# Where the streamed tiles of a transformer block's matmuls begin in on-chip memory: from one offset for all to steps of 32 bytes

## The chip, the cores and the metric

The kernel is one program on one core of one Trainium2 chip. A core has a matmul engine (TensorE, PE in the profile, with its weight loads as PEld), a vector engine (VectorE, DVE), a scalar engine (ScalarE, ACT), a general engine (GpSimd, POOL) and an engine that issues transfers (SyncE, SP). They share an on-chip memory of 128 partitions; sums of products are built up in a second one, the accumulator memory. The metric is device time in microseconds, from the first to the last instruction of the core; lower is better.

## The reference

The computation is one layer of a diffusion block in float32, for one sequence of 512 tokens of 2048 features, with a context of 256 tokens. Cut to what matters here:

```python
sh1, sc1, g1, sh2, sc2, g2 = split(silu(c) @ w_ada + b_ada)      # modulation; the same for the context
h  = rmsnorm(x + pos, norm_mix_pre) * (1 + sc1) + sh1            # [512, 2048]
z, xbc, dt, hy = split(h @ w_in)                                 # 2048 -> 5664
y  = concat([ssd(z, xbc, dt, context), hyena(hy)]) @ w_out       # 2048 -> 2048
x  = x + pos + g1 * rmsnorm(y, norm_mix_post)
h  = rmsnorm(x, norm_ffn_pre) * (1 + sc2) + sh2
x  = x + g2 * rmsnorm((silu(h @ w_gate) * (h @ w_up)) @ w_down, norm_ffn_post)   # 2048 -> 5632 -> 2048
```

Nearly all arithmetic lies in the products with `w_in`, `w_out`, `w_gate`, `w_up` and `w_down`.

## The kernel before

**Tiles.** Features lie on the 128 partitions and tokens along them, so a tensor of 2048 features is 16 blocks `k`, each a tile of 128 x 512 (2048 bytes in a partition). A product is taken in float32 with split operands: `x = xh + xl` and `w = wh + wl`. For each block, `mm3` issues three matmuls into one accumulator: `wh` against `xh`, `wh` against `xl`, `wl` against `xh`. In each the weights (128 x 128) are loaded into the array, and the tile of `x` is streamed through it; this text calls it the moving tile. `gemm` goes through the 16 blocks in order, so that two pieces of weights of 8 blocks each make one output tile.

**Names.** The moving tiles have several names over the program, in the same slots: `hh`/`hl` (the normed input), `mh`/`ml` (the mixed output before `w_out`) and `fh`/`fl` (the input of the feed-forward part) are tiles of pool `big`, tags `h0` to `h15` and `l0` to `l15`. `ah`/`al` are the activations that `w_down` takes: six slots each in pool `fa`. `ch`/`cl` are the context, 256 tokens. A few pieces of weights that are used twice go into slots of `big` as well (`bhi`/`blo`, by `wload_big`).

**Weights.** `wload` brings a raw piece of 128 x 1024 by a transfer from SP, ScalarE casts it to `whi` and VectorE (GpSimd in the start) makes `wlo`; raw, `whi` and `wlo` have three buffers each. A piece is split two pieces ahead of its use (`push`).

**Order.** The program's order is written out by hand. Products follow each other; small steps of other work (norms, the state-space part, the transforms of the long convolution, the later modulation vectors) are generators in the lists `urgent` and `fillers`, of which `pump` runs some after every fourth block. Each engine then takes its instructions in order, except for what the build may move where two tiles of different lifetimes share memory: a tile that needs the place of an earlier one waits until that one is released.

**Places in memory.** Pools are laid out one behind the other, on the left side upwards: `cst` (constants), `big`, `wp` (weights), `rsm`, and above them the pools of each part. As built, before the change, every tile of `big` begins at 96 modulo 256 bytes of a partition, and so do `raw`, `whi` and `wlo`, with a slice of weights every 512 bytes; `ah`, `al`, `ch` and `cl` begin at 32 modulo 256.

Of the kernel before, what the change touches and what calls it, by code (L numbers as in the profile page):

```python
# [46 lines left out]
# columns of the packed per-feature vectors  # L47
# [17 lines left out]
def block_kernel(ctx: ExitStack, tc: tile.TileContext, I: dict, out: bass.AP, dbg=None, stop=None):  # L65
# [32 lines left out]

    uniq = [0]
# [18 lines left out]
    mod = cst.tile([128, 8, 16], F32, name="mod")  # L118
    nc.gpsimd.memset(ones, 1.0)
# [4 lines left out]
    hh = [big.tile([128, 512], F32R, tag=f"h{k}", name=f"hh{k}") for k in range(KT)]  # L124
    hl = [big.tile([128, 512], F32R, tag=f"l{k}", name=f"hl{k}") for k in range(KT)]
    hx = [(hh[k], hl[k]) for k in range(KT)]

# [38 lines left out]
    def wload_big(ap, q):  # L166
        """Into the slots of four blocks of features that are free meanwhile."""
        raw = wraw(ap)
        parts = []
        for i in range(2):  # L170
            o = i * 512
            hi = big.tile([128, 512], F32R, tag=f"h{q * 2 + i}", name=nm("bhi"))
            lo = big.tile([128, 512], F32R, tag=f"l{q * 2 + i}", name=nm("blo"))
            split(hi, lo, raw[:, o : o + 512])
            parts += [(hi[:, c : c + 128], lo[:, c : c + 128]) for c in range(0, 512, 128)]
        return parts
# [11 lines left out]
    # a piece is split some pieces before its products are issued  # L188
# [11 lines left out]
    def flush(nxt=()):  # L200
        """Issue what waits; the first pieces of the next part are split meanwhile."""
        nxt = list(nxt)
        while ahead or nxt:
            if nxt:
                stash.append(wload(nxt.pop(0)))
            if ahead:
                w, fn = ahead.pop(0)
                fn(w)
# [28 lines left out]
    class Sumsq:  # L237
        """Sum over the features of the squares, by partitions first; the last ones go to the PE alone."""
# [91 lines left out]
    # mod slots: shift and scale of x, then of ctx; the four later sections of x  # L330
# [6 lines left out]
    # =====================================================================  # L337
    # start: x + pos, its norm, and h by blocks of features as w_ada arrives;
    # six tiles of the first GEMM take each block as it comes
    # =====================================================================  # L340
# [11 lines left out]
    # silu(c) and silu(c_ctx) on every partition  # L352
# [22 lines left out]
    # the scales, of x and ctx at once: rows of w_ada on the PE  # L375
# [22 lines left out]
    # the shifts: silu(c) and silu(c_ctx) against transposed blocks of w_ada  # L398
# [11 lines left out]
    # sums of squares: half of the features on the PE, the others on DVE first  # L410
# [56 lines left out]
    # =====================================================================  # L467
    # xbc of x, and the first hyena inputs; beside them the modulation of ctx
    # =====================================================================
# [57 lines left out]
    def u_out(pv, px, j):  # L527
# [10 lines left out]
        # folded again: sums and differences of the even, then of the odd part  # L538
# [17 lines left out]
    # ctx: norm and modulation  # L556
# [23 lines left out]
    # dt: of x from the third tile of the start  # L580
# [42 lines left out]
    # =====================================================================  # L623
    # ctx: dt and its part of the xbc GEMM
    # =====================================================================
# [25 lines left out]
    def softplus():  # L651
        # softplus(x) = max(x, 0) + log1p(e), e = exp(-|x|); log1p(e) = 2 atanh(e / (2 + e))
# [46 lines left out]
    def hb8(ap):  # [128, 8] over heads of 64  # L699
        return ap.unsqueeze(2).broadcast_to([128, 8, 64])  # L700
# [4 lines left out]
    def decayed(td, x, c, d, g):  # dt * x, with the decay up to the end of the chunk  # L705
        o = d * 16 + g * 8
        tt(nc.gpsimd, v8(td), v8(x), hb8(dd[:, c, o : o + 8]), MUL)
        return td
# [11 lines left out]
    # =====================================================================  # L720
    # SSD, beside the GEMMs of the hyena inputs
    # =====================================================================
# [45 lines left out]
    # the steps of dt * A in two parts of 12 bits, and masks of ones that both parts meet exactly  # L768
# [13 lines left out]
    # of four heads: the terms of the sums of dt * A, and dt of the direction that a pair of steps belongs to  # L782
# [16 lines left out]
    def ssd():  # L799
        for g in range(2):  # L800
# [19 lines left out]
            for c in range(4):  # L820
# [20 lines left out]
                for q4 in range(2):  # L841
                    # the exponents of both directions do not meet: one is zero where the other is not
# [68 lines left out]
    # =====================================================================  # L911
    # z, the gate of the SSD output; beside it the transform of the hyena
    # filter, by quarters of the channels
    # =====================================================================
# [68 lines left out]
    def filt():  # L983
        for q in range(4):
# [20 lines left out]
            # h1 at t = 0 is in the norm, but not in the filter  # L1005
# [6 lines left out]
            # times t and 512 - t meet: sums serve the even cosines and odd sines,  # L1012
            # differences the others; the first row holds the times 0 and 256
# [43 lines left out]
    mh = [big.tile([128, 512], F32R, tag=f"h{k}", name=f"mh{k}") for k in range(KT)]  # L1057
    mlo = [big.tile([128, 512], F32R, tag=f"l{k}", name=f"ml{k}") for k in range(KT)]
# [4 lines left out]
    # the norm's factor of each token multiplies the product with w_out instead  # L1063
# [6 lines left out]
    # =====================================================================  # L1070
    # w_out, the SSD half of the sum; beside it the hyena: x1 * v, its
    # transform, product, inverse; then * x0
    # =====================================================================
# [13 lines left out]
    def chain():  # L1087
        for q in range(4):
# [6 lines left out]
            for m in range(4):  # L1095
                pc = aux()
                for s, tab in ((0, ucos), (1, usin)):
                    # even frequencies meet only the sums or only the differences
# [66 lines left out]
    # =====================================================================  # L1165
    # w_out, the hyena half, by halves of the tokens; beside it and the first
    # FFN tiles: residual, norm and modulation before the FFN
    # =====================================================================
# [4 lines left out]
    posc = fa.tile([128, 512], F32, tag="ah", bufs=NA, name="posc")  # L1173
    pos = pos_load(jn, posc.rearrange("p (k c) -> p k c", k=8))
# [13 lines left out]
    def junction(h, prs):  # L1188
# [10 lines left out]
        for k in range(KT):  # L1199
            if h == 0:  # L1200
                fx[k] = (big.tile([128, 512], F32R, tag=f"h{k}", name=f"fh{k}"),
                         big.tile([128, 512], F32R, tag=f"l{k}", name=f"fl{k}"))
            modulated(fx[k][0][:, sl], fx[k][1][:, sl], yT[k][:, sl], a2[:, k : k + 1], mod[:, 5, k : k + 1], rx[:, sl], 256)
            yield
# [20 lines left out]
    # the second half takes first the pieces that are still there from the first  # L1225
# [15 lines left out]
    # =====================================================================  # L1241
    # FFN
    # =====================================================================
    acts = {}

    def gate_up(i, c0, c1):
# [3 lines left out]
        def up_done(pu):  # L1250
            if i not in acts:
                h = fa.tile([128, 512], F32R, tag="ah", bufs=NA, name=nm("ah"))
                l = fa.tile([128, 512], F32R, tag="al", bufs=NA, name=nm("al"))
# [72 lines left out]
    # the pieces stay for the second half: most in the place of the FFN's input  # L1326
# [14 lines left out]
def _constants():  # L1341
# [4 lines left out]
    def emb(n):  # L1346
        a = (np.arange(n, dtype=f)[:, None] * om).astype(np.float64)
        return np.concatenate([np.sin(a), np.cos(a)], -1).astype(f)  # [n, 1024]
# [11 lines left out]
    # times 0 .. 255, then 256, 511, 510, ... 257  # L1360
# [7 lines left out]
    # frequencies: multiples of 4, the other even ones, the odd ones  # L1368
# [11 lines left out]
    ph = (m.T * (2 * tp[None, :] + 1)) % 2048  # [m, t'], in units of pi / 1024  # L1380
# [4 lines left out]
    for name, u in (("cos", uc), ("sin", us)):  # L1385
        near, far = u[:, :128], u[:, :127:-1]
        odd = [x[lo : lo + 128] / 2 for lo in (256, 384) for x in (near + far, near - far)]
        blocks = np.stack([near[:128], near[128:256]] + odd, 0)  # [block, m, t]
# [6 lines left out]
def _layout(a):  # L1395
# [4 lines left out]
    def stat(w):  # [K, N] -> [N/128, K/1024, 128, 8 * 128]  # L1400
# [3 lines left out]
    def cols(v):  # [n * 128] -> [128, n]  # L1404
# [12 lines left out]
    # [pc, k2, 128, sec, g, 512] -> [sec, g, pc, 128, k2, 512]  # L1417
    wa = a["w_ada"][0]
    R["ada2"] = wa.reshape(8, 2, 128, 6, 4, 512).transpose(3, 4, 0, 2, 1, 5).reshape(6, 4, 8, 128, 1024)[1:]
    # the first section transposed: [half, 1024, k, 128] -> [k, half, 128, 1024]  # L1420
# [3 lines left out]
    # [chunk, k4, 128, q, s, 128] -> [chunk, q, 128, s, k4, 128]  # L1424
# [30 lines left out]
```

## Time and profile before

| | |
|---|---|
| time, median of 2 runs | 2626.44 us (2624.69 to 2628.19) |
| the profiled execution, first to last instruction | 2627.0 us, the execution's own time as the trace has it |
| matmuls / share of the span that PE is busy | 12196 / 96% |
| weight loads (PEld) | 78% |
| VectorE, ScalarE, GpSimd | 56%, 29%, 17% |
| transfers | 388.52 MB, mean 148 GB/s |

Matmuls are pipelined: the record of one lasts longer than the step from its start to the start of the next, and it is this step that adds up to the time. A step is therefore read from the starts in the timeline, as the difference of two starts over the number of matmuls between them, and not from the mean duration in a group of instructions.

### The profile page before, as it was taken

What the parts mean: (1) busy time and instruction counts of PE and PEld (TensorE: products, weight loads), DVE (VectorE), ACT (ScalarE), POOL (GpSimd) and SP (SyncE); (2) the same over time, 40 slices, a digit from 0 to 9 for tenths busy, and PEclk for the clock granted to TensorE, in tenths of its full rate; (3) what the DMA queues carried; (4) which work ended last, traced back from release to release, by engine and by line L of the source; (5) the groups of instructions that cost most, each with busy time, mean ns of one, the idle gap of its engine ahead of it and who ended that gap; (6) DMA issues with size and microseconds to landing.
All of it is one profiled execution on the core that took longest, in us unless ns stands there. A gap on an engine that the chain in (4) does not pass through costs nothing.

```text
span 2627.0 us, 30945 instructions
## 1 busy us (share of the span) xinstructions
PE 2525.5 (96%) x12196; PEld 2050.2 (78%) x12196; DVE 1471.1 (56%) x1889; ACT 758.2 (29%) x1062; POOL 454.2 (17%) x421
## 2 busy tenths in 40 slices
PE   8999999899999999999999999999999999999996
PEld 3467779577767788889888888888888888888886
DVE  7986756888878766696334343434343333333336
ACT  3143325222123322454322222222222222222224
POOL 1230010565523245740000000000000000000005
PEclk9999999899999999999999999999999999999998
DMA  8867644445356666345433333333333333333232
GB/s 288 317 211 237 224 159 167 145 147 162 112 196 209 245 223 221 103 147 185 145 112 112 108 110 112 112 111 112 112 112 105 96 96 96 96 96 94 95 103 80
DMA packets 129354, 388.52 MB, mean 148 GB/s; under 512 B 13775, under 2 KB 34703, under 8 KB 127672
## 3 DMA queue, kind: packets, MB, share of 16 engines
q1 hardware_dynamic: 129208, 386.54, 44.9%
q8 instruction: 96, 1.57, 0.2%
q14 instruction: 50, 0.41, 0.0%
HBM read 367.09 MB, written 19.40 MB: 147 GB/s over the span
## 4 chain that ended last, share of the span: by engine, by line
PE 54%; DVE 2%; issue 0%; POOL 0%; ACT 0%; POOLq 0%; DVEq 0%; ACTq 0%
PE acc L82 54%; DVE y2a L79 1%; DVE wlo L79 1%; DVE yTa L76 0%; POOL gs L79 0%; DVE yTa L79 0%; DVE fl L76 0%; PE aux L82 0%; DVE mt L76 0%; ACT whi L162 0%; PE aux L234 0%; POOL r L79 0%; POOL yTa L79 0%; ACT sq L73 0%; ACT dg L73 0%
## 5 line engine op out<-in xcount | busy, mean ns | idle before, releaser
L162 ACT CAST whi<-raw 128x1024 fp32r<-128x1024 f32 (+1 forms) x436 | 452.9, 1039 | 1424.2 <-PE acc L82 1185.3
L79 DVE TENSOR_TENSOR wlo<-raw,whi 128x1024 fp32r<-128x1024 f32 x420 | 530.8, 1264 | 544.4 <-ACT whi L162 540.5
L82 PE MATMUL acc<-fh,wlo 128*128 128x512 f32 (+1 forms) x1600 | 581.9, 364 | 5.3 <-DVE wlo L79 5.3
L82 PE MATMUL acc<-fh,whi 128*128 128x512 f32 (+1 forms) x1600 | 582.4, 364 | 0.1
L82 PE MATMUL acc<-fl,whi 128*128 128x512 f32 (+1 forms) x1600 | 581.9, 364 | 0.1
L82 PEld LDWEIGHTS acc<-fh,wlo 128*128 128x128 f32 x1600 | 301.8, 189 | 53.8 <-DVE wlo L79 6.1
L82 PEld LDWEIGHTS acc<-fl,whi 128*128 128x128 f32 x1600 | 301.8, 189 | 47.8 <-DVE fl L76 0.3
L82 PEld LDWEIGHTS acc<-fh,whi 128*128 128x128 f32 x1600 | 301.8, 189 | 47.8 <-ACT fh L73 0.3
L79 POOL TENSOR_TENSOR gs<-gs,sq 128x256 f32<-128x256 f32 x91 | 85.6, 944 | 1457.6 <-ACT sq L73 1454.1
L82 PE MATMUL acc<-hh,whi 128*128 128x512 f32 x688 | 287.0, 419 | 4.4 <-ACT hh L73 4.2
L82 PE MATMUL acc<-hl,whi 128*128 128x512 f32 x688 | 278.5, 405 | 2.8 <-DVE hl L76 2.8
L82 PE MATMUL acc<-hh,wlo 128*128 128x512 f32 x688 | 278.1, 404 | 0.0
L82 PE MATMUL acc<-ah,whi 128*128 128x512 f32 (+1 forms) x688 | 265.7, 386 | 0.0
L82 PE MATMUL acc<-ah,wlo 128*128 128x512 f32 (+1 forms) x688 | 265.5, 386 | 0.0
L82 PE MATMUL acc<-al,whi 128*128 128x512 f32 (+1 forms) x688 | 265.4, 386 | 0.0
L76 DVE SCALAR_TENSOR_TENSOR ada<-raw,cc,ada 128x512 f32<-128x512 f32 x240 | 200.5, 835 | 114.0 <-DMA raw<-in_ada 111.0
L79 DVE TENSOR_TENSOR y2a<-y2a,acc 128x512 f32<-128x512 f32 (+1 forms) x176 | 112.0, 638 | 210.5 <-PE acc L82 209.4
L82 PEld LDWEIGHTS acc<-hh,whi 128*128 128x128 f32 x688 | 135.0, 197 | 40.6 <-ACT hh L73 6.1
L82 PEld LDWEIGHTS acc<-hl,whi 128*128 128x128 f32 x688 | 135.3, 197 | 34.6 <-DVE hl L76 3.8
L82 PEld LDWEIGHTS acc<-hh,wlo 128*128 128x128 f32 x688 | 134.0, 195 | 34.6 <-issue 4.5
L82 PEld LDWEIGHTS acc<-ah,wlo 128*128 128x128 f32 x688 | 128.7, 187 | 29.8
L82 PEld LDWEIGHTS acc<-ah,whi 128*128 128x128 f32 x688 | 128.6, 187 | 29.7 <-ACT ah L179 0.2
(297 smaller groups left out, 3074.4 us busy)
## 6 DMA issues: line engine op xcount, KB each, us to landing
raw<-in_ada SPq DMA_DIRECT2D x128, 512.0 KB, 3.7
raw<-in_w_gate SPq DMA_DIRECT2D x100, 512.0 KB, 3.5
raw<-in_w_up SPq DMA_DIRECT2D x100, 512.0 KB, 3.5
raw<-in_w_down SPq DMA_DIRECT2D x88, 512.0 KB, 3.5
ada<-in_ada SPq DMA_DIRECT2D x64, 512.0 KB, 4.8
raw<-in_w_hy SPq DMA_DIRECT2D x44, 512.0 KB, 3.7
raw<-in_w_out SPq DMA_DIRECT2D x41, 512.0 KB, 4.0
raw<-in_w_xbc SPq DMA_DIRECT2D x38, 512.0 KB, 3.4
```

What stands on the lines that cost most here:

```text
L76: nc.vector.scalar_tensor_tensor(out=o, in0=a, scalar=s, in1=b, op0=op0, op1=op1)
L79: e.tensor_tensor(out=o, in0=a, in1=b, op=op)
L82: nc.tensor.matmul(o, lhsT, rhs, start=start, stop=stop)
L162: nc.scalar.copy(out=hi[:, :n], in_=raw[:, :n])
```

## The change

Every tile of `big`, and `ah` and `al`, is allocated 520 columns wide and used in its first 512, so that neighbouring tiles are 2080 bytes apart instead of 2048. Two small tiles that nothing uses (`pad0`, `pad1`) shift the pools behind them, and a scratch area at the foot of the memory, for descriptors of transfers that GpSimd would issue, is cut from 16 KB to 1 KB; no transfer of this kernel is issued there. As built, block `k` of `hh`, `hl`, `mh`, `ml`, `fh`, `fl` then begins at 32 `k` modulo 256; `raw`, `whi` and `wlo` begin at 0; slot `i` of `ah` begins at 32 `i`, of `al` at 192 + 32 `i`; `ch` and `cl` begin at 0. Comments are dropped too, which shifts line numbers by two.

```diff
+    rsm.tile([128, 16], F32, name="pad1")
...
     mod = cst.tile([128, 8, 16], F32, name="mod")
+    cst.tile([128, 40], F32, name="pad0")
...
-    hh = [big.tile([128, 512], F32R, tag=f"h{k}", name=f"hh{k}") for k in range(KT)]
-    hl = [big.tile([128, 512], F32R, tag=f"l{k}", name=f"hl{k}") for k in range(KT)]
+    hh = [big.tile([128, 520], F32R, tag=f"h{k}", name=f"hh{k}")[:, 0:512] for k in range(KT)]
+    hl = [big.tile([128, 520], F32R, tag=f"l{k}", name=f"hl{k}")[:, 0:512] for k in range(KT)]
...
-            hi = big.tile([128, 512], F32R, tag=f"h{q * 2 + i}", name=nm("bhi"))
-            lo = big.tile([128, 512], F32R, tag=f"l{q * 2 + i}", name=nm("blo"))
+            hi = big.tile([128, 520], F32R, tag=f"h{q * 2 + i}", name=nm("bhi"))[:, 0:512]
+            lo = big.tile([128, 520], F32R, tag=f"l{q * 2 + i}", name=nm("blo"))[:, 0:512]
... (the same for mh, ml, fh, fl)
-                h = fa.tile([128, 512], F32R, tag="ah", bufs=NA, name=nm("ah"))
-                l = fa.tile([128, 512], F32R, tag="al", bufs=NA, name=nm("al"))
+                h = fa.tile([128, 520], F32R, tag="ah", bufs=NA, name=nm("ah"))[:, 0:512]
+                l = fa.tile([128, 520], F32R, tag="al", bufs=NA, name=nm("al"))[:, 0:512]
...
-    nc = _bacc.Bacc("TRN2", target_bir_lowering=False, num_devices=1)
+    nc = _bacc.Bacc("TRN2", target_bir_lowering=False, num_devices=1, dynamic_dma_scratch_size=1024)
```

The matmuls keep their order, all of them, and so do VectorE's instructions. Between the start and the first products of `w_xbc` the pools on the left now overlap less with those on the right, and some instructions of the other engines change places.

GpSimd, where the start ends: `gs` is the running sum of squares of the context, `eo` and `f` are the folded hyena input, which TensorE transposes next. Before:

```order
L79 TENSOR_TENSOR gs_1530<-gs_1530,sq_1551 128x256
L79 TENSOR_TENSOR eo_1196<-hv_1186 128x256 x2
L79 TENSOR_TENSOR gs_1530<-gs_1530,sq_1556 128x256
L79 TENSOR_TENSOR f_267_1199<-eo_1196 128x2x128 x2
L79 TENSOR_TENSOR gs_1530<-gs_1530,sq_1635 128x256
L79 TENSOR_TENSOR gs_1530<-gs_1530,sq_1640 128x256
```

and now:

```order
L79 TENSOR_TENSOR gs_1532<-gs_1532,sq_1553 128x256
L79 TENSOR_TENSOR gs_1532<-gs_1532,sq_1558 128x256
L79 TENSOR_TENSOR gs_1532<-gs_1532,sq_1637 128x256
L79 TENSOR_TENSOR eo_1198<-hv_1188 128x256 x2
L79 TENSOR_TENSOR gs_1532<-gs_1532,sq_1642 128x256
L79 TENSOR_TENSOR f_267_1201<-eo_1198 128x2x128 x2
```

Two additions to `gs` now stand ahead of `f`.

ScalarE, at the same place: `whi` is a piece of weights, `xct` a tile of the context that has just been loaded. Before:

```order
L73 ACTIVATE ea<-bc 128x32
L162 CAST whi_1087<-raw_1085 128x1024
L73 ACTIVATE CT_1118<-acc_318,vec 128x512
L73 ACTIVATE CT_1119<-acc_319,vec 128x512
L73 ACTIVATE BT_1116<-acc_320,vec 128x512
```

and now:

```order
L73 ACTIVATE ea<-bc 128x32
L73 ACTIVATE gs_1532<-xct_1530 128x256
L73 ACTIVATE sq_1536<-xct_1534 128x256
L164 CAST whi_1089<-raw_1087 128x1024
L73 ACTIVATE CT_1120<-acc_320,vec 128x512
```

The first two squares of the context stand ahead of the second cast. SP issues the transfers of the context's tiles and of the masks a few places earlier there.

## Rows read from the trace of the kernel before

**Rows 1.** The page: PE's share, its 40 slices.
```profile
PE 2525.5 (96%) x12196; PEld 2050.2 (78%) x12196; DVE 1471.1 (56%) x1889; ACT 758.2 (29%) x1062; POOL 454.2 (17%) x421
...
PE   8999999899999999999999999999999999999996
```
**Rows 2.** A stretch: start:end, length; PE, PEld, DVE, ACT, POOL busy (count); PEclk, DMA.
```profile
1900.00:2000.00 100.00, 100.00 (x437) 81.58 (x436) 39.90 (x44) 21.44 (x23) 0.00 (x0) 1.00 0.34 107
```
**Rows 3.** Groups of PE's instructions by shape: count, busy us, mean ns, idle before.
```profile
L82 PE MATMUL acc<-fh,whi 128*128 128x512 f32 x1216 | 473.4, 389 | 0.0
...
L82 PE MATMUL acc<-hh,whi 128*128 128x512 f32 x688 | 287.0, 419 | 4.4 <-ACT hh L73 4.2 <-ACT hx L73 0.2
...
L82 PE MATMUL acc<-ah,whi 128*128 128x512 f32 x640 | 252.2, 394 | 0.0
...
L82 PE MATMUL acc<-fh,whi 128*128 128x256 f32 x384 | 108.9, 285 | 0.1
...
L82 PE MATMUL acc<-mh,whi 128*128 128x256 f32 x192 | 55.4, 289 | 1.4 <-DVE yTa L79 1.4
...
L82 PE MATMUL acc<-mh,whi 128*128 128x512 f32 x128 | 54.6, 426 | 0.0
...
L82 PE MATMUL acc<-ch,whi 128*128 128x256 f32 x176 | 50.2, 285 | 0.0
...
L82 PE MATMUL acc<-ah,bhi 128*128 128x256 f32 x80 | 22.5, 281 | 1.5 <-DVE y2a L79 1.5
...
L82 PE MATMUL acc<-mh,bhi 128*128 128x256 f32 x64 | 18.2, 284 | 0.0
...
L82 PE MATMUL acc<-ah,whi 128*128 128x256 f32 x48 | 13.5, 285 | 0.0
```
**Rows 4.** Timeline of PE, gate and up products: start us, length; 195 matmuls apart.
```profile
1854.93 0.39 PE L82 MATMUL acc<-fh,whi 128*128 128x512 f32 x1
...
1899.13 0.39 PE L82 MATMUL acc<-fh,whi 128*128 128x512 f32 x1
```
**Rows 5.** Timeline of PE, down products; 161 matmuls apart.
```profile
1812.25 0.39 PE L82 MATMUL acc<-ah,whi 128*128 128x512 f32 x1
...
1849.82 0.39 PE L82 MATMUL acc<-ah,wlo 128*128 128x512 f32 x1
```
**Rows 6.** Timeline of PE, gate and up by halves of the tokens; 166 matmuls apart.
```profile
1199.96 0.28 PE L82 MATMUL acc<-fl,whi 128*128 128x256 f32 x1
...
1219.88 0.28 PE L82 MATMUL acc<-fh,wlo 128*128 128x256 f32 x1
```
**Rows 7.** Timeline of PE, products of the context; 122 matmuls apart.
```profile
402.10 0.28 PE L82 MATMUL acc<-ch,wlo 128*128 128x256 f32 x1
...
415.93 0.28 PE L82 MATMUL acc<-cl,whi 128*128 128x256 f32 x1
```
**Rows 8.** Timeline of PE, start products 23 matmuls apart; the transposes of `f`.
```profile
183.67 0.39 PE L82 MATMUL acc<-hh,whi 128*128 128x512 f32 x1
...
188.88 0.39 PE L82 MATMUL acc<-hh,wlo 128*128 128x512 f32 x1
189.12 0.60 PE L548 MATMUL aux<-ident,f 128*128 128x128 f32 x4
```
**Rows 9.** Timeline of PE, products with w_out; 10 matmuls apart, then two-pass float32.
```profile
921.85 0.40 PE L82 MATMUL acc<-ml,whi 128*128 128x512 f32 x1
...
924.15 0.40 PE L82 MATMUL acc<-mh,wlo 128*128 128x512 f32 x1
...
925.70 0.59 PE L82 MATMUL aux<-eot,ucos 128*128 128x256 f32 x2
926.13 0.59 PE L82 MATMUL aux<-eot,usin 128*128 128x256 f32 x2
```
**Rows 10.** Waits of PE from 150 to 420 us: us in total, times, longest.
```profile
PE aux L548 <- POOL f L79: 10.1, 8, 2.4
```
**Rows 11.** Timeline of GpSimd: the first folded tile.
```profile
179.10 1.88 POOL L79 TENSOR_TENSOR f<-eo 128x256 f32<-128x256 f32 x2
```

More of the change, by code (lines that the diff above doesn't have):

```diff
@@ L1056, in block_kernel @@
     flush(I["w_out"][n, 0] for n in range(2))
-    mh = [big.tile([128, 512], F32R, tag=f"h{k}", name=f"mh{k}") for k in range(KT)]
-    mlo = [big.tile([128, 512], F32R, tag=f"l{k}", name=f"ml{k}") for k in range(KT)]
+    mh = [big.tile([128, 520], F32R, tag=f"h{k}", name=f"mh{k}")[:, 0:512] for k in range(KT)]
+    mlo = [big.tile([128, 520], F32R, tag=f"l{k}", name=f"ml{k}")[:, 0:512] for k in range(KT)]
     for j in range(8):
@@ L1172, in block_kernel @@
     jn = jn_cm.__enter__()
-    posc = fa.tile([128, 512], F32, tag="ah", bufs=NA, name="posc")
-    pos = pos_load(jn, posc.rearrange("p (k c) -> p k c", k=8))
+    posc = fa.tile([128, 520], F32, tag="ah", bufs=NA, name="posc")
+    pos = pos_load(jn, posc[:, 0:512].rearrange("p (k c) -> p k c", k=8))
     xr = [jn.tile([128, 512], F32, name=f"xr{k}") for k in range(KT)]
@@ L1200, in junction @@
             if h == 0:
-                fx[k] = (big.tile([128, 512], F32R, tag=f"h{k}", name=f"fh{k}"),
-                         big.tile([128, 512], F32R, tag=f"l{k}", name=f"fl{k}"))
+                fx[k] = (big.tile([128, 520], F32R, tag=f"h{k}", name=f"fh{k}")[:, 0:512],
+                         big.tile([128, 520], F32R, tag=f"l{k}", name=f"fl{k}")[:, 0:512])
             modulated(fx[k][0][:, sl], fx[k][1][:, sl], yT[k][:, sl], a2[:, k : k + 1], mod[:, 5, k : k + 1], rx[:, sl], 256)
```

## The prediction

> **What bounds the kernel now.** I read the page first, then stretches of the span, then PE's groups, then the timeline. The page shows PE busy for 96% and in 9 tenths of nearly every slice [rows 1]. A busy matmul engine need not be at its peak, so the next view is a stretch in the feed-forward part: PE is busy for all of its 100 us, at the full granted clock of 1.00, while VectorE, ScalarE, GpSimd and the transfers have room [rows 2]. Nothing that another engine does can shorten this part. What counts is the step from the start of one matmul to the start of the next.
>
> The groups give the numbers of matmuls; each row stands for three kinds of equal count, xh and xl with the high weights and xh with the low ones [rows 3]. With 512 columns there are 3 x 1216 = 3648 on `fh`/`fl`, 3 x 640 = 1920 on `ah`/`al`, and 3 x (688 + 128) = 2448 on `hh`/`hl` and `mh`/`ml`. With 256 columns there are 3 x (384 + 192 + 64) = 1920 on tiles of `big`, and 3 x (176 + 80 + 48) = 912 on `ch`/`cl` and `ah`/`al`.
>
> The timeline gives the steps, as differences of starts:
> - `fh`, 512 columns: 44.20 us over 195, 226.7 ns [rows 4].
> - `ah`, 512 columns: 37.57 us over 161, 233.4 ns [rows 5].
> - `fh`, 256 columns: 19.92 us over 166, 120.0 ns [rows 6].
> - `ch`, 256 columns: 13.83 us over 122, 113.4 ns [rows 7].
> - `hh` in a quiet stretch: 5.21 us over 23, 226.5 ns [rows 8].
> - `mh` just after other work broke the chain: 2.30 us over 10, 230.0 ns [rows 9].
>
> 512 columns at 2.4 GHz are 213.3 ns, 256 are 106.7. So the kept steps lie 13.3, 20.0, 13.3 and 6.7 ns above the streaming time: 2, 3, 2 and 1 times the time of 16 columns. The same instruction on the same shape costs 3% more on `ah` than on `fh`, and on 256 columns it is the other way round. What differs is where the moving tile begins: 96 modulo 256, as the weights, or 32. After a break the step is neither of the two. I read this as a chain that falls into a regular step, one of several, according to where its tiles begin and where it was disturbed, and keeps it as long as nothing changes. The step is from rows; its cause is my reading.
>
> **The change, part by part.** No matmul is added or taken away and their order stays, so the change is worth what it does to these steps, on 8016 matmuls of 512 columns and 2832 of 256, nearly all on the path. Two percent of the time is 52.5 us (about what a measurement can tell from no change); spread over the 8016 that would be 6.5 ns each.
>
> *The offsets.* The trace shows no tile whose offset to the weights changes from block to block. Now it changes after every three matmuls, so I expect that no regular step lasts, and take for 512 columns the step of the chain that has just been broken, 230.0 ns [rows 9], the nearest row. For 256 columns no such row stands here and I take the middle of the two kept steps, 116.7 ns.
> - `fh`/`fl`: 3648 x (230.0 - 226.7) = +12.0 us.
> - `ah`/`al`: 1920 x (230.0 - 233.4) = -6.5 us.
> - `hh`, `mh`: these run beside much other work; I take half of them as kept at 226.5 [rows 8] and half as broken at 230.0 [rows 9], now 228.25 in the mean: 2448 x 1.75 = +4.3 us.
> - 256 columns of `big`: 1920 x (116.7 - 120.0) = -6.3 us.
> - 256 columns of `ch`, `ah`: 912 x (116.7 - 113.4) = +3.0 us.
>
> Sum +6.5 us. The bounds are the kept steps. If every chain finds the short one (226.7 and 113.4): 0, -12.9, -3.8, -12.7, 0, together -29 us. If every one falls into the long one (233.4 and 120.0): +24.4, 0, +12.6, 0, +6.0, together +43 us. That lies inside two percent either way.
>
> *The moved instructions.* They cost nothing in my sum. The folded tile `f` is finished at 180.98 us [rows 11] and TensorE takes it at 189.12 [rows 8]: 8.1 us of cover for two additions and what they wait for. Beyond that cover the price is the kind of wait that TensorE has for `f` today, 10.1 us over eight waits, the longest 2.4 [rows 10]; I bound it by 0 and +2.4 us. The cast behind the two squares of the context waits for a transfer that SP now issues no later than before; the same bound holds. A gain of the same size is possible too, since the context is loaded earlier.
>
> *The scratch area.* No transfer is issued by GpSimd, so nothing uses it: 0.
>
> The sum is made on the profiled execution, 2627.0 us, 0.6 above the median of the runs: 2633.5, and 2633 on the median's scale.
>
> **The rivals.**
>
> *The place does not matter.* Then the time stays at 2627 us. Against it stand 226.7 and 233.4 ns for equal instructions; for it, that the two come in different parts of the program with different weights. Chance 0.10. The Trainium skill, "SBUF — State Buffer", section "Who interferes with whom", says that PE and ACT never wait on anyone: by that rule no placement of tiles could change a step, and the change would be worth 0 us where the rows give bounds of -29 to +43. The 6.7 ns between rows 4 and 5 speak against taking it that far.
>
> *Part of the excess is a ragged edge.* The excess comes in multiples of 6.7 ns, the time in which 16 columns or 64 bytes of a partition are streamed, and every moving tile so far begins at 32 modulo 64. A tile that begins in the middle of 64 bytes touches one such piece more than one that begins on the edge. Half of the blocks now begin on an edge: a mean of 3.3 ns less on 8016 + 2832 matmuls is -36 us, 2591 us. Nothing in the trace has an aligned moving tile, so it can be neither shown nor excluded. Chance 0.14.
>
> *The excess is a clash of moving tile and weights, and the spread ends it.* If both streams take pieces of the memory in turn, tiles at one common distance clash in every matmul, and tiles spread over eight offsets may avoid it. How low a step can go is seen on matmuls that stream at half the rate: two passes of 256 columns follow the next two after 0.43 us [rows 9], 215 ns for each, 1.7 ns above 2 x 106.7. With 215 for 512 columns and 108.4 for 256: 3648 x 11.7 + 1920 x 18.4 + 2448 x 13.3 + 1920 x 11.6 + 912 x 5.0 = 42.7 + 35.3 + 32.6 + 22.3 + 4.6 = 137 us, so 2490 us; if half of the blocks come free of it, 2559 us. For it speaks that the excess depends on the distance at all; against it that a different distance gave one step more on 512 columns and one less on 256, so no distance seen is free. Chance 0.23, most of it nearer the half. The Trainium skill, "TensorE: Matmul & The Clock Gate", section "Wait — 56ns, not 53.3ns?", gives a step of N / 2.4 + 2.5 ns, 215.7 for 512 columns, as a floor whatever the tile's place. The chain of `fh` stays 11 ns above it, so by that figure the room is there, about 130 us, but the page says nothing of what takes it.
>
> *The spread adds clashes.* One mechanism on the other side: the distance between moving tile and weights now runs through all values, so every chain meets the bad ones, and each matmul loses one piece more than in the worst kept step: 240.0 ns for 512 columns and 126.7 for 256. That is 3648 x 13.3 + 1920 x 6.6 + 2448 x 11.75 + 1920 x 6.7 + 912 x 13.3 = 48.5 + 12.7 + 28.8 + 12.9 + 12.1 = +115 us, 2742 us. It decides from a mean step of 235.3 ns on 512 columns (the present mean is 228.8, and 6.5 ns is two percent). For it: the step of `ah`, at another distance, is the longer. Against it: no stretch read here stays above 233.4. Chance 0.08.
>
> **The numbers.** The chance of my forecast is what is left, 0.45, at 2633 us, its own range 2598 to 2670. Faster by over two percent is below 2574 us: nearly all of the third rival and a tail of the second, 0.25. Slower by over two percent is above 2679: the last rival, 0.08. Within two percent: 0.67. The range reaches up to the upper bound of the forecast, 2670, and leaves out the last rival; down it goes to 2540, into the third rival, and leaves out about half of it, so that some 2 in 10 are outside.
>
> **What would show it.** In the timeline after, the same stretches: the first and last start of `fh`, `ah` and `hh` chains over their count. Steps that change from block to block with a mean near 230 confirm the forecast; a steady 226.7 on everything its lower bound. Steps that alternate by 6.7 ns with even and odd blocks would show the ragged edge. Steps near 216 to 220 on `fh` and `ah` alike would show that the clash is gone, and my reading of the broken chain wrong; 240 on every block the last rival. PE must still be busy for all of each late stretch; if it is not, a wait has come in that I have not seen. A longer wait of TensorE for `f` near 190 us would show that the moved instructions cost.

## The result, and the profile after

The changed kernel takes 2647.39 us (median of two runs, 2645.33 to 2649.45) against 2626.44 us before, a ratio of 1.0086 with a 95% interval from 1.0068 to 1.0105. It is slower by 0.9%: less than the two percent of the forecast's bound, but outside the interval of no change. The profiled execution's span is 2647.7 us, 20.7 us more than before.

The page of the changed kernel, PE's share and its 40 slices, answers to [rows 1]:

```profile
PE 2552.7 (96%) x12196; PEld 2053.3 (78%) x12196; DVE 1468.0 (55%) x1889; ACT 758.7 (29%) x1062; POOL 454.5 (17%) x421
...
PE   8999989899999999999999999999999999999997
```

Nothing is seen here but that PE's busy time has grown by 27.2 us with the same 12196 matmuls. The same stretch as in [rows 2], with the same columns:

```profile
1900.00:2000.00 100.00, 100.00 (x433) 81.06 (x433) 39.78 (x44) 21.49 (x23) 0.00 (x0) 1.00 0.35 111
```

PE is busy all the time, at the full granted clock, and still starts 433 matmuls in 100 us where it started 437. No wait and no clock has come in; the steps are longer. The timeline of PE shows them (columns: start, duration, engine, line, operation, out<-in, weights, moving tile, type, count). Shown are the first and last starts of one chain of `hh` with the transposes of `f` behind it, of one of `ch` with 256 columns, one of `fh` with 256, and then `ah`, `fh` and `ah` with 512:

```profile
170.70 0.40 PE L82 MATMUL acc<-hl,whi 128*128 128x512 f32 x1
...
186.97 0.40 PE L82 MATMUL acc<-hh,wlo 128*128 128x512 f32 x1
187.21 0.60 PE L550 MATMUL aux<-ident,f 128*128 128x128 f32 x4
...
401.74 0.28 PE L82 MATMUL acc<-ch,wlo 128*128 128x256 f32 x1
...
415.77 0.28 PE L82 MATMUL acc<-ch,wlo 128*128 128x256 f32 x1
...
1199.96 0.28 PE L82 MATMUL acc<-fh,whi 128*128 128x256 f32 x1
...
1219.84 0.28 PE L82 MATMUL acc<-fh,whi 128*128 128x256 f32 x1
...
1818.29 0.40 PE L82 MATMUL acc<-ah,whi 128*128 128x512 f32 x1
...
1862.87 0.40 PE L82 MATMUL acc<-ah,wlo 128*128 128x512 f32 x1
1863.10 0.40 PE L82 MATMUL acc<-fh,whi 128*128 128x512 f32 x1
...
1900.07 0.40 PE L82 MATMUL acc<-fh,whi 128*128 128x512 f32 x1
...
1905.65 0.40 PE L82 MATMUL acc<-fh,whi 128*128 128x512 f32 x1
...
1911.23 0.40 PE L82 MATMUL acc<-fh,whi 128*128 128x512 f32 x1
...
1952.15 0.39 PE L82 MATMUL acc<-fh,wlo 128*128 128x512 f32 x1
1952.38 0.39 PE L82 MATMUL acc<-ah,whi 128*128 128x512 f32 x1
...
1996.41 0.40 PE L82 MATMUL acc<-ah,wlo 128*128 128x512 f32 x1
```

`fh`, 512 columns: 89.05 us over 383 matmuls, 232.5 ns, where [rows 4] gave 226.7. `ah`: 44.58 us over 191, 233.4 ns, and in the next chain 44.03 over 191, 230.5 ns; a third chain, from 2086.82 to 2131.13 us, takes 232.0. Each chain goes through four of the six slots, and the three means come back in this order; over the whole run the mean is 232.0 where [rows 5] gave 233.4. `hh`: 16.27 us over 70, 232.4 ns, against 226.5 in [rows 8]. With 256 columns `fh` takes 19.88 us over 168, 118.3 ns, against 120.0 in [rows 6], and `ch` 14.03 over 117, 119.9 ns, against 113.4 in [rows 7]. The rows at 1900.07, 1905.65 and 1911.23 are 24 matmuls apart each, eight blocks: 5.58 us both times. The single steps between them run from 226 to 238 ns, and the same 24 steps come back every eight blocks.

Summed over the whole run, each start-to-start difference booked under the matmul that begins it:

| step | before, us | after, us | difference | forecast |
|---|---|---|---|---|
| `fh`/`fl`, 512 columns | 827.5 | 848.4 | +20.9 | +12.0 |
| `ah`/`al`, 512 | 448.0 | 445.4 | -2.6 | -6.5 |
| `hh`/`hl`, `mh`/`ml`, 512 | 631.1 | 638.6 | +7.5 | +4.3 |
| 256 columns of `big` | 247.2 | 246.1 | -1.2 | -6.3 |
| 256 columns of `ch`, `ah` | 115.4 | 117.8 | +2.5 | +3.0 |
| all other matmuls and waits | 337.8 | 331.7 | -6.0 | 0 |
| sum | 2607.0 | 2628.0 | +21.0 | +6.5 |

The moved instructions can be read from PE's waits between 150 and 420 us (waiter and releaser: total us, times, longest us), which answer to [rows 10]:

```profile
PE aux L550 <- POOL f L79: 8.9, 8, 2.3
```

and from the timeline of POOL, which answers to [rows 11]:

```profile
176.81 1.89 POOL L79 TENSOR_TENSOR f<-eo 128x256 f32<-128x256 f32 x2
```

`f` is done at 178.70 us and TensorE takes it at 187.21: the cover is 8.5 us and was 8.1. PE's waits for `f` are 1.2 us shorter in total. The moved instructions cost nothing.

### The profile page after: what moved, and what is told of

It is laid out like the page before. It is cut to its first block, busy times and chain, and to the rows that moved or that the text cites. A ratio compares the mean times of both kernels' runs of the same rounds, so it can differ in the third digit from the quotient of the medians.

```text
span 2647.7 us, 30944 instructions
## 1 busy us (share of the span) xinstructions
PE 2552.7 (96%) x12196; PEld 2053.3 (78%) x12196; DVE 1468.0 (55%) x1889; ACT 758.7 (29%) x1062; POOL 454.5 (17%) x421
## 4 chain that ended last, share of the span: by engine, by line
PE 73%; DVE 14%; issue 4%; POOL 4%; DMA 3%; ACT 1%; SPq 0%; POOLq 0%; DVEq 0%; ACTq 0%
PE acc L82 68%; PE aux L82 4%; DVE jk L407 2%; DVE wlo L79 2%; DVE ada L76 2%; DMA raw<-in_ada 1%; DVE arl L79 1%; DVE y2a L79 1%; DMA ada<-in_ada 1%; DVE mt L76 1%; DVE E L79 1%; PE aux L1127 1%; POOL f L79 0%; ACT whi L164 0%; POOL gs L79 0%
## 5 line engine op out<-in xcount | busy, mean ns | idle before, releaser
L82 PE MATMUL acc<-fh,wlo 128*128 128x512 f32 (+1 forms) x1600 | 588.6, 368 | 5.5 <-DVE wlo L79 5.5
L82 PE MATMUL acc<-fh,whi 128*128 128x512 f32 (+1 forms) x1600 | 589.8, 369 | 0.1
L82 PEld LDWEIGHTS acc<-al,whi 128*128 128x128 f32 x688 | 129.3, 188 | 28.6
```

The lines of the kernel that those rows point to most:

```text
L82: nc.tensor.matmul(o, lhsT, rhs, start=start, stop=stop)
```

## The experiments

The theory to be tested is that of the forecast: what matters is how far the moving tile lies from the weights, modulo 256 bytes, and a distance that changes from block to block has a longer mean step than distance 0. The rivals are a price that hangs on the place of the tile itself (the ragged edge), a clash that depends on how long the loads of weights are, the wider pitch, and the moved instructions.

**The steps by themselves.** The layer is replaced by lone chains of matmuls with nothing beside them. The weights `wh` and `wl` begin at 0 modulo 256, eight moving tiles `xa` to `xh` at 0, 32, ... 224. The chains `ca` to `ch` keep one tile each, `ha` to `hh` the same with 256 columns, `sa` goes one tile further with each block as the change does, `sb`, `sd` and `sc` two, four and three, and `ta`, `tb`, `td` are their forms with 256 columns; `d` has the second matmul's tile elsewhere than that of the first and third. Each block is the three matmuls of `mm3`:

```diff
+    xs = [sb.tile([128, 520], F32R, name="x" + c) for c in "abcdefgh"]
+        for k, (i, j) in enumerate(blocks):
+            nc.tensor.matmul(p[:, :n], wh[:, o : o + 128], xs[i][:, 0:n], start=f, stop=False)
+            nc.tensor.matmul(p[:, :n], wh[:, o : o + 128], xs[j][:, 0:n], start=False, stop=False)
+            nc.tensor.matmul(p[:, :n], wl[:, o : o + 128], xs[i][:, 0:n], start=False, stop=l)
+    run("c" + "abcdefgh"[i], 512, [(i, i)] * 24, 128 + 4 * r)
+    run("s" + c, 512, [(k * s % 8, k * s % 8) for k in range(64)], 128)
```

> Leaves out the whole layer: only matmuls of the same form (three per block, 24 blocks a chain, weights at 0 modulo 256 bytes) on tiles at eight distances from the weights, 0 to 224 in steps of 32; four chains for each distance, begun after a short matmul of 128, 132, 136 or 140 columns; then chains whose block moves by 32, 64, 96 or 128 bytes. Theory of the kept step: at a constant distance every chain settles after a few matmuls and then keeps a step that is a multiple of 6.7 ns (226.7 or 233.3 for 512 columns, 113.3 or 120.0 for 256), at every distance; which of them depends on how it began. A distance that moves by 32 keeps none: mean 232 to 233 as in the changed kernel, repeating every 24 matmuls. Rival, a price for each distance: each of the eight distances has one step of its own whatever came before, their mean is 232.5 (the changed kernel's mean on fh), distance 0 gives 231.4 (mean of its block 0), 32 gives 230.8. Rival, the edge: distances 0, 64, 128, 192 are 6.7 ns shorter than 32, 96, 160, 224.

The timeline of PE in this run shows the chains at distance 0 (`ca`, with its beginning) and 32 (`cb`), two of the chains of 256 columns at 192 (`hg`), the chain that moves by 32 bytes (`sa`) and its form with 256 columns (`ta`):

```profile
21.22 0.39 PE L94 MATMUL ca<-xa,wh 128*128 128x512 f32 x1
...
22.38 0.39 PE L93 MATMUL ca<-xa,wh 128*128 128x512 f32 x1
...
26.01 0.39 PE L94 MATMUL ca<-xa,wh 128*128 128x512 f32 x1
...
26.46 0.39 PE L93 MATMUL ca<-xa,wh 128*128 128x512 f32 x1
...
27.14 0.39 PE L93 MATMUL ca<-xa,wh 128*128 128x512 f32 x1
...
36.89 0.39 PE L94 MATMUL ca<-xa,wh 128*128 128x512 f32 x1
...
91.91 0.39 PE L94 MATMUL cb<-xb,wh 128*128 128x512 f32 x1
...
103.11 0.39 PE L94 MATMUL cb<-xb,wh 128*128 128x512 f32 x1
...
769.22 0.28 PE L95 MATMUL hg<-xg,wl 128*128 128x256 f32 x1
...
774.66 0.28 PE L95 MATMUL hg<-xg,wl 128*128 128x256 f32 x1
...
777.59 0.28 PE L95 MATMUL hg<-xg,wl 128*128 128x256 f32 x1
...
783.25 0.28 PE L95 MATMUL hg<-xg,wl 128*128 128x256 f32 x1
...
840.30 0.39 PE L94 MATMUL sa<-xh,wh 128*128 128x512 f32 x1
...
840.76 0.40 PE L93 MATMUL sa<-xa,wh 128*128 128x512 f32 x1
...
841.46 0.40 PE L93 MATMUL sa<-xb,wh 128*128 128x512 f32 x1
...
879.36 0.39 PE L94 MATMUL sa<-xh,wh 128*128 128x512 f32 x1
...
1016.38 0.28 PE L94 MATMUL ta<-xh,wh 128*128 128x256 f32 x1
...
1036.26 0.28 PE L94 MATMUL ta<-xh,wh 128*128 128x256 f32 x1
```

`ca` takes 10.88 us over 48 matmuls, 226.7 ns; `cb` 11.20 over 48, 233.3; `sa` 39.06 over 168, 232.5; `ta` 19.88 over 168, 118.3. The two chains of `hg` differ only in what came before them: 5.44 us over 48, 113.3 ns, and 5.66 over 48, some 118. The steps of `sa` and `ta` are those of `fh` in the changed kernel, to the tenth of a nanosecond, with no other work beside them. All means, in ns (two where the beginning decided):

| distance, bytes | 0 | 32 | 64 | 96 | 128 | 160 | 192 | 224 |
|---|---|---|---|---|---|---|---|---|
| 512 columns | 226.7 | 233.3 | 228.9 | 233.3 | 232.4 | 234.3 | 233.3 | 233.3 |
| 256 columns | 120.0 | 116.7 | 117.8 | 120.0 | 118.8 | 118.6 or 117.3 | 113.3 or 117.8 | 118.3 |

Of these distances with 512 columns, 0 is the only one with one even, short step; at the others the steps run through a short cycle (231, 235, 233, 234 ns, for example, at 32), and at 192 two of the four beginnings gave an even 233.3. The means are not all multiples of 6.7 ns apart, as the theory had it. With one tile for the three matmuls and 512 columns, the mean came out the same for each of the four beginnings that were tried, so what happened before the chain did not pick it. Elsewhere it did. With 256 columns one beginning of the four gave 113.3 at 192 and the others 117.8, and at 160 one gave 117.3 and the others 118.6. In `d`, where the second matmul's tile lies at another distance than the first's and third's, 512 columns gave 233.3 after one beginning and 231.1 after the other at 32 and at 128, and 231.1 and 232.2 at 160. So the theory that a disturbance chooses among kept steps is refuted for the one form and shown for the others. The single steps depend on what came before in the one form too: the block of `xa` takes 0.68 us for three matmuls in `ca` (26.46 to 27.14) and 0.70 in `sa` (840.76 to 841.46). So the mean of a moving chain is not a plain sum of prices either, although the mean of the eight, 231.9, comes near to 232.5. Moving by 64, 96 or 128 bytes gave 231.7, 231.4 and 232.2; for 128 the mean of its two distances would be 229.5.

**Everything 96 bytes further.** The same chains, with every tile at 96 bytes more, so that the distances are kept and the places are not:

```diff
-    base = sb.tile([128, 32], F32, name="base")
+    base = sb.tile([128, 56], F32, name="base")
```

> The same chains with everything, weights and tiles, moved up by 96 bytes, so that what began on an edge of 64 bytes does not any more; the rest of the layer is left out here too. Theory of the kept step: the same steps at the same distances, since only the distance and the beginning of the chain count. The edge: chains on tiles at odd and even places change roles, by 6.7 ns. A price for each distance: unchanged.

All means equal those of the first run within 0.05 ns, and where a beginning had decided, the same one decided the same way. Between place and distance it is the distance that counts; the ragged edge, which is a matter of the place alone, is refuted.

**Everything at distance 0.** The changed kernel with tiles of 512 columns, and so with its pads, its scratch area and the instructions that moved where the start ends; beside the products with `w_out` some instructions of the engines other than TensorE change places once more:

```diff
-    hh = [big.tile([128, 520], F32R, tag=f"h{k}", name=f"hh{k}")[:, 0:512] for k in range(KT)]
+    hh = [big.tile([128, 512], F32R, tag=f"h{k}", name=f"hh{k}")[:, 0:512] for k in range(KT)]
... (the same for hl, mh, ml, fh, fl, ah, al and the weights in slots of big)
```

> The changed kernel with tiles of 512 columns again: every moving tile and all weights begin at 0 modulo 256, one distance, 0, for all, and on an edge of 64 bytes. Kept step: fh 226.7 ns as before, ah 226.7 (it was 233.4 at another distance) or 233.3 if it begins badly, ch 120.0 instead of 113.4; together -13 to 0 us on ah and +6 us on 912 matmuls of 256 columns: 2619 to 2633 us. Edge: 6.7 ns less on 10848 matmuls, -72 us: 2555 us. A price for each distance, 231.4 at distance 0: fh +17, ah -4, hh and mh +8: about 2647 us.

2611.99 us, ratio 0.9944 [0.9930, 0.9957]. In the timeline of PE, one chain of `fh` and the one of `ah` behind it:

```profile
1841.51 0.39 PE L82 MATMUL acc<-fh,whi 128*128 128x512 f32 x1
...
1928.33 0.39 PE L82 MATMUL acc<-fh,wlo 128*128 128x512 f32 x1
1928.55 0.39 PE L82 MATMUL acc<-ah,whi 128*128 128x512 f32 x1
...
1971.85 0.39 PE L82 MATMUL acc<-ah,wlo 128*128 128x512 f32 x1
```

86.82 us over 383 and 43.30 over 191: 226.7 ns for both. `ah`/`al` lose 12.8 us against before. The loss of the change is all in the spread; taken alone, the rest of it (pads, order, scratch area) comes with a gain, most of it because `ah` now lies at distance 0. My expectation was too high by 7 us at its lower end. In this profile the other matmuls and waits are 5.6 us shorter than before, the same unexplained term as in the table above.

**Only `ah` moved, in the kernel before.** A pad of 64 bytes ahead in the pool of `ah`/`al`, and nothing else; their distance to the weights goes from 192 to 0:

```diff
+    fa.tile([128, 16], F32, name="padf")
```

> The kernel before with 64 bytes of padding ahead of ah and al, so that they too begin at the weights' own offset, 96 modulo 256; nothing else moves. Kept step: ah goes from 233.4 to 226.7 ns, 1920 x 6.7 = -12.9 us, and its 384 matmuls of 256 columns from 113.4 to 120.0, +2.5 us: 2616 us, ratio 0.996. A price for each distance says the same for ah if distance 0 costs 226.7 wherever it stands, but then block 0 of the changed kernel should cost it too, and it costs 231.4. The place does not matter: 2626 us.

2617.66 us, ratio 0.9962 [0.9949, 0.9976], as expected. A chain of `ah` in PE's timeline:

```profile
1926.02 0.39 PE L82 MATMUL acc<-ah,whi 128*128 128x512 f32 x1
...
1969.31 0.39 PE L82 MATMUL acc<-ah,wlo 128*128 128x512 f32 x1
```

43.29 us over 191, 226.6 ns, where it was 233.4 [rows 5]. One line that moves 12 tiles by 64 bytes is worth 10 us. `ah` with 256 columns takes 1.5 us more, as the price of distance 0 in the table has it.

This run also shows a kept step in the kernel itself. `ch` was not touched: it lies where it lay and its matmuls come in the same order, but the chain that took 113.4 ns in the kernel before [rows 7] took 14.13 us over 120, 117.8 ns, here:

```profile
396.44 0.28 PE L82 MATMUL acc<-cl,whi 128*128 128x256 f32 x1
...
410.57 0.28 PE L82 MATMUL acc<-cl,whi 128*128 128x256 f32 x1
```

These are the two means of distance 192 in the table; which of them a chain gets was not the place's doing.

**Finer distances, narrower weights, fewer columns.** Lone chains again. `fa` to `fi` move the tile by 4 bytes each, from 0 to 32; `ma` and `mb` load 32 columns of weights instead of 128; others place the low weights elsewhere, or stream from 128 to 504 columns:

```diff
+    for c in (0, 1, 2, 3, 4, 5, 6, 7, 8):
+            run("f" + "abcdefghi"[c], 512, c, 128, 128 + 8 * r, wl)
+    for c, s in ((0, "a"), (8, "b"), (16, "c"), (48, "d")):
+        run("m" + s, 512, c, 32, 128, wl)
```

> Leaves out the layer again. Chains at one constant distance, by 4 bytes from 0 to 32; chains with 32 or 64 columns of weights instead of 128; chains in which only the low weights begin elsewhere (0 to 224); chains of 128 to 504 columns. Theory, a clash between the loads of the weights and the moving tile: with 32 columns of weights the step falls to 213.3 + 2 ns at every distance, with 64 it falls part of the way; the low weights' place moves the step of the triple. Rival, the moving tile alone (its own start and end against the one before): 226.7 to 233.3 ns stay with short weights, and the low weights' place changes nothing. Of the finer distances: if only whole pieces of 16 or 32 bytes count, 4, 8 and 12 bytes keep 226.7; else they spread between 226.7 and 234.

The timeline of PE shows the distances 4 and 28 bytes (`fb`, `fh`), and 32 columns of weights at distance 0 (`ma`):

```profile
60.61 0.40 PE L96 MATMUL fb<-xa,wh 128*128 128x512 f32 x1
...
71.97 0.40 PE L96 MATMUL fb<-xa,wh 128*128 128x512 f32 x1
...
263.29 0.39 PE L96 MATMUL fh<-xa,wh 128*128 128x512 f32 x1
...
274.17 0.39 PE L96 MATMUL fh<-xa,wh 128*128 128x512 f32 x1
...
330.03 0.40 PE L96 MATMUL ma<-xa,wh 128*32 128x512 f32 x1
...
341.15 0.40 PE L96 MATMUL ma<-xa,wh 128*32 128x512 f32 x1
```

Over 48 matmuls each: 236.7 ns, 226.7 and 231.7. From 0 to 32 bytes the means are 226.7, 236.7, 233.3, 228.9, 231.7, 236.1, 233.3, 226.7 and 233.3: the order is not one of near and far. With 32 columns the record of one load lasts 0.11 us instead of 0.19, and this did not bring 215 ns: the step at distance 0 became 5 ns longer, and at 32, 64 and 192 bytes it was 233.3, 231.7 and 231.7 where the table has 233.3, 228.9 and 233.3. With 64 columns of weights the four were 230.0, 230.8, 228.3 and 232.7. So the clash in its simple form, an excess that grows with what the loads read, is refuted. The low weights count too: at distances 32 to 224 from the high ones they gave 231.1 to 233.3 where 226.7 stood. 504 columns took 226.7 as 512 do, and 192 took 111.7 as 128 do. Nothing came below 226.7 on 512 columns.

**A wider pitch without the spread.** The changed kernel with tiles of 576 columns, 2304 bytes or nine times 256:

```diff
-    hh = [big.tile([128, 520], F32R, tag=f"h{k}", name=f"hh{k}")[:, 0:512] for k in range(KT)]
+    hh = [big.tile([128, 576], F32R, tag=f"h{k}", name=f"hh{k}")[:, 0:512] for k in range(KT)]
... (the same for the others)
```

> The changed kernel with tiles 576 columns wide: blocks 2304 bytes apart, so all at 0 modulo 256 again, the same distance to the weights for all, but wider apart than in the change. What costs is the distance modulo 256: then fh keeps 226.7 ns and ah 226.7, and the time is that of tiles of 512 columns at 0, about 2612 us. What costs is that blocks no longer lie one behind the other: then fh stays near 232.5 ns, about 2647 us.

2613.33 us, ratio 0.9956 [0.9943, 0.9970]. A chain of `fh` in PE's timeline:

```profile
1844.19 0.39 PE L82 MATMUL acc<-fh,whi 128*128 128x512 f32 x1
...
1931.00 0.39 PE L82 MATMUL acc<-fh,wlo 128*128 128x512 f32 x1
```

86.81 us over 383, 226.7 ns. It is not the gap between the tiles but the distance modulo 256. By its trace every engine has its instructions in the order of the kernel before, so the moves where the start ends are not in it.

**The spread on `ah` alone.** The changed kernel with 512 columns in `big` and 520 in `ah`/`al`; the edit is that of the kernel with everything at distance 0, without its lines on `ah` and `al`.

> The changed kernel with the tiles of pool big 512 columns wide again (all at 0 modulo 256) and ah, al still 520. By the terms of the two traces fh, hh and mh give back 20.9 + 7.5 us and ah stays at 232.0 ns: 2647 - 28 = about 2619 us, fh at 226.7 ns. If the chains of ah hand their disorder on to those of fh, fh does not come back to 226.7 at once and the time lies between 2619 and 2647.

2625.09 us, ratio 1.0002 [0.9993, 1.0012]. PE's timeline, one chain of `fh` and the next of `ah`:

```profile
1852.39 0.40 PE L82 MATMUL acc<-fh,whi 128*128 128x512 f32 x1
...
1939.24 0.39 PE L82 MATMUL acc<-fh,wlo 128*128 128x512 f32 x1
1939.46 0.40 PE L82 MATMUL acc<-ah,whi 128*128 128x512 f32 x1
...
1983.51 0.40 PE L82 MATMUL acc<-ah,wlo 128*128 128x512 f32 x1
```

`fh` is back at 226.8 ns (86.85 us over 383), `ah` stays spread, 230.6 here and 232.0 in the mean. All its instructions stand in the changed kernel's order. The part that costs against the kernel before is the spread of `big`: 1.0086 with it, 1.0002 without. The spread of `ah` costs too, against distance 0 (1.0002 and 0.9944), but `ah` came from 233.4. The total is 6 us above what was expected. In its profile 512 columns stand as forecast and the matmuls of 256 columns take 6.4 us more than before (2.7 on `fh`, 2.6 on `ch`, 1.1 on `ah`, nothing on `mh`), which I had not put in.

**Distance 0, and the context at 192.** The kernel with everything at distance 0, and a pad of 192 bytes ahead of `ch`/`cl`:

```diff
+    chp.tile([128, 48], F32, name="padc")
```

> All moving tiles and weights at 0 modulo 256, but ch and cl, whose matmuls have 256 columns, at 192 (the distance that they had before the change). In the lone chains 256 columns took 120.0 ns at distance 0 and 113.3 or 117.8 at 192: 528 x 2.2 to 6.7 ns = 1.2 to 3.5 us less than with everything at 0, 2608 to 2611 us, faster than both kernels. If a fixed distance of 0 is best for all, 2612 us or more.

2611.45 us, ratio 0.9945 [0.9933, 0.9958]. The matmuls on `ch`/`cl` take 66.4 us in its profile, 2.7 less than without the pad, but the total cannot be told from 0.9944. By these ratios both versions are some 0.55% faster than the kernel before, and 1.4% faster than the changed one (0.9945 over 1.0086).

## Why the prediction was right, and which term was off

The forecast was 2633 us, the likeliest of its cases, and the measured 2647 lies in that case's own range, 2598 to 2670, within two percent. The direction was right; the size was not: +21 us where the sum said +6.5.

- **What bounds the kernel** was read rightly: PE is busy for all of the late stretch, and a few nanoseconds in each step make up the whole difference.
- **That an offset that changes from block to block has no even step** was right, and so was the place of the loss: all five signs in the table came as forecast. The two signs of 256 columns carry little: the 1920 matmuls of `big` take 246.1 us here, and 246.1 to 249.9 in the five kernels tried that leave them at distance 0. The reason behind it was half wrong. I had chains pick a step by how they were disturbed and keep it. For 512 columns on one tile the lone chains show a mean for each distance, whatever came before; for 256 columns at 192 chains do pick, 113.3 or 117.8, in the lone chains and in the kernel.
- **The mis-sized term** is the step of 512 columns. I took 230.0 ns from ten matmuls behind a break [rows 9]; it is 232.5 on `fh`, 232.4 on `hh` and 232.0 on `ah`. With 2.5 ns more on 3648 matmuls `fh`/`fl` come to 12.0 + 9.1 = +21.1 us (+20.9 measured), and with 2.0 more `ah`/`al` to -2.7 (-2.6 measured). The row was not of the thing that it stood for: its ten matmuls lie at the constant distance 0, and their steps are 234, 235, 225, 230, 236, 229, 232, 231, 227 and 226 ns, a chain on its way back to its even step. `ca` begins in the same way: 1.16 us over 5 matmuls, 232 ns, then 3.63 over 16, 226.9. That the mean of such a beginning lies within 2.5 ns of the moving chain's is luck.
- **The steps of 256 columns**: 116.7 was the middle of two values of constant distances. `fh` takes 118.3 and `ch` 119.9, so the gain on `big` was 1.2 us and not 6.3.
- **The moved instructions** cost nothing, as forecast; PE's cover of `f` was there. The kernel at distance 0 keeps them and the one with the wider pitch does not, and they come to the same, 0.9944 and 0.9956.
- **The rest**, -6.0 us, was not forecast. The same term is 3.1 to 5.6 us below that of the profile before in all five full kernels tried; the one with the single pad moves no instruction, and there it is -4.4. So it doesn't come from the moved instructions; whether that one profile was long there by chance was not tried. In the profile with the single pad `hh`, which stayed in its place, is 6.7 us shorter too, so terms of this size come with the execution. Without it the five terms of the offsets come to +27, four times the sum.

The rivals: *the place does not matter* is refuted by 64 bytes of pad that change `ah` from 233.4 to 226.6 ns. The rule of the Trainium skill, "SBUF — State Buffer", section "Who interferes with whom", by which PE never waits on anyone, does not say what placement does to a step. The lone chains, with no other engine at work, show that the difference is between PE's own streams. *The ragged edge* fell with the shift of 96 bytes, which changed nothing. *The clash that the spread ends* did not come: of nine finer distances, eight coarse ones and four ways to move, none went below 226.7 ns. The Trainium skill, "TensorE: Matmul & The Clock Gate", section "Wait — 56ns, not 53.3ns?", would give 215.7 ns for 512 columns. No chain of 512 columns here reached it. *The spread adds clashes* had the right sign, but the mean came to 232.5 and not to the 235.3 from which it would decide.

Open is what the 13.3 ns above the streaming time at distance 0 are. They are not a price per column: the finer chains give the same 13.3 on 320 columns (146.7 ns) and 384 (173.3) as on 256 and 512, and 16.0 to 16.7 on 448 to 504. Open too is why the mean goes up and down with 4 bytes, and what lets a chain of 256 columns settle on one of two means. Not tried were other spacings of the slices of weights, and other types of data.

## What to carry to other kernels

Where matmuls follow each other without a gap, the place of the moving tile against the weights was worth 3% of a step here (226.7 against 233.4 ns, 236.7 at the worst), so read the steps from starts in the timeline, one chain for each pair of pools, before looking for anything else. With 512 columns of split float32 put moving tiles and both kinds of weights at the same place modulo 256 bytes, and keep all blocks there; the spread over eight distances brought about their mean (232.5 ns, and 231.9). Price a new step by a row of the same kind that holds a whole cycle of it, not by the beginning of another chain, and measure it alone in a short chain where there is none: the lone chain gave 232.5 ns, the kernel 232.5.

## What was unexpected of the hardware

- The mean step of equal matmuls depends on the distance between moving tile and weights, not on the place: 226.7 to 236.7 ns with 512 columns, 113.3 to 120.0 with 256.
- At some distances it also depends on what came before: 113.3 or 117.8 ns with 256 columns at 192, kept for the whole chain, and in the kernel for 135 matmuls.
- It is not monotonic: 4 bytes gave 236.7 ns, 12 bytes 228.9, 28 bytes 226.7, 32 bytes 233.3.
- The best distance differs with the number of columns: 0 is the best for 512 (226.7, as at 28 bytes) and, with 96, the worst for 256 (120.0); at 192 it is 233.3 for 512, and 113.3 or 117.8 for 256.
- Loads of 32 columns of weights made the step at distance 0 longer, 231.7 ns and not 226.7.
